# A two-layer decoder trunk on one core: the value projection cut in two, two more pairs of heads turned by DMA, copies moved off GpSimd, and a softmax written with a minimum

## The chip, the cores and the metric

The kernel runs on 1 core of a Trainium2 chip. The time is the device time of one execution in microseconds (us). The engines are TensorE (matmuls; PE in the profile, PEld for its weight loads), VectorE (DVE), ScalarE (ACT), GpSimd (POOL) and SyncE (SP), which here only issues DMAs. The kernel before took 558.63 us (median of 3 runs, 558.53 to 558.71).

## The reference

The model has 256 positions of width 1024 and two layers. Layer 0 mixes positions with a chunked gated MLP, layer 1 with attention of 16 heads of width 64. Each mixer is followed by a gated MLP with a causal convolution of width 3, and each of the four sub-layers ends in `x <- LayerNorm(alpha * x + f(x))`. Everything is float32.

What the change touches is the attention of layer 1. With 256 positions there is one key block, so each query sees its own block alone, under the causal mask and with a bias by distance:

```
qkv = (x @ w_qkv).reshape(B, S, 3, H, Dh)
s   = q * Dh**-0.5 @ k.T + bias[head, bucket(t - j)]      # -inf where j > t
p   = softmax(s)
o   = p @ v                                               # (S, H * Dh)
x   = layer_norm(alpha * x + o @ w_o, g, b)
```

## The kernel before

**Arithmetic.** A float32 product is built from three products of reduced-precision parts. Each operand is split into a high part and a low part (`split`, line 404): one copy on ScalarE or VectorE rounds to the high part, and one subtraction on VectorE gives the low part. A step of a projection is then high x high, high x low and low x high, all summed in one bank of PSUM. The weights are split in the same way as they arrive: `prep` (line 476) loads a 1 MB chunk into one of two raw buffers, ScalarE writes `whi` and VectorE writes `wlo`, 1024 columns at a time.

**The stream of weights.** All weight chunks stand in one list, `stream` (line 422), in the order of their use. The kernel holds five chunks (`CHUNKS`). When a chunk has been used, `spent` (line 514) starts the load and the split of the chunk five places further on. The attention stage uses four chunks of the value weights (`b_v`), then eight of query and key weights (`b_qk`, one chunk for one pair of heads), then four of the output projection (`b_o`).

**The planner.** The program does not write the order of the instructions directly. Every operation is recorded with an engine, a cost in ns, and what it reads and writes (`Plan.op`, line 96). `schedule` (line 178) then simulates the five engines with these costs and the order of each engine's instructions is what comes out. TensorE's operations are of two sorts. Bulk ones (the projections) keep the order in which they were recorded. Those marked `fill` (scores, products with the values, transposes) are put in between at the first moment when the simulation has their data ready. On the other engines the operation with the earliest due time goes first, and the due time is worked back from TensorE's operations. Once the order is fixed each engine runs its own instructions strictly in that order and waits on semaphores: where the chip is later than the simulation, the engine stands. A DMA is simulated as 1100 ns plus its bytes at 360 bytes per ns (line 236), and 910 ns later (line 91) its data count as there.

**The attention stage** (`moba`, line 998):

- The value projection comes first (lines 1018 to 1030): for each of 8 slices of the inner dimension and each half t of the positions, two outputs of 512 columns. Slices 0 to 4 are done for both halves, then 5 to 7. It holds four banks of PSUM (both tiles of two banks, `twos`). The second half of the positions is still being normalised and transposed when this projection begins; the first 30 matmuls are of the first half.
- `project(i)` (line 1033) computes queries and keys of pair i of heads, 16 matmuls of 512 columns and 16 of 256. `part` reads the two banks and splits the results.
- In the middle of the projection of pairs 2, 4 and 6 stand the scores of the two pairs before (`scores`, line 1059), and behind these the products with the values of the two pairs before those (`also`).
- `softmax` (line 1087) works in two pieces per head, 128 and 256 columns wide. VectorE adds the bias to the scores, reversed along the columns, and takes the maximum; a tiny VectorE instruction negates both maxima; ScalarE computes the exponential with that as its bias and sums it; VectorE takes the reciprocal and scales.
- The probabilities must be transposed before they meet the values. Pairs 0 to 3 (`BY_XBAR`) go through `turn_apart` (line 1113): a copy brings the low and the high 16-bit halves of the floats apart, a DMA transposes both planes of 16-bit elements, and a copy joins them. Of the two heads of a pair one goes by GpSimd and one by ScalarE, in both copies. Pairs 4 to 7 are transposed on TensorE (`turn`, line 1140), three 128 x 128 blocks for each head, and ScalarE copies the result out of PSUM.
- `apply` (line 1163) multiplies with the values; `keep` splits the result for the output projection.
- After the projection of pair 7 come the scores of pair 6 with the transposes of pairs 4 and 5, and the scores of pair 7 with the products of 4 and 5. The transposes and products of pairs 6 and 7 are placed behind given lengths of the output projection's matmuls (2600, 5800 and 9300 ns, lines 1193 and 1194).

**The output projection** (`project_out`, line 758, with `b_o`) has 8 slices, one for each pair of heads. It starts with slices 0 and 1, so the later pairs are needed only after a good part of its matmuls. Its four banks are given out in the order of `free` (line 765).

**Normalisation** (`stats`, line 614): after the statistics on VectorE one GpSimd instruction raises the variance to the power -1/2. The planner counts it as 465 ns (line 627).

Of the kernel before, what the change touches and what calls it, by code (L numbers as in the profile page):

```python
# [14 lines left out]
AF = mybir.ActivationFunctionType  # L15
# [4 lines left out]
P = 128  # L20
D = 1024
# [34 lines left out]
BY_XBAR = (0, 1, 2, 3)  # L56
# [207 lines left out]
def trunk_kernel(ctx: ExitStack, tc: tile.TileContext, a: dict, out: bass.AP):  # L264
# [163 lines left out]
    stream += [("b_v", c) for c in range(4)]  # L428
    stream += [("b_qk", c) for c in range(8)]
    stream += [("b_o", c) for c in range(4)]  # L430
# [183 lines left out]
    def stats(r, x, cuts, sum_into=None):  # L614
# [12 lines left out]
        plan.op("pool", 465, lambda: nc.gpsimd.tensor_tensor(rstd, ve, nhalf.ap, op=ALU.pow),  # L627
# [130 lines left out]
    def project_out(name, nk, at, xold, li, rows_i):  # L758
# [6 lines left out]
        free = [bank(True) for _ in range(2 * NT)]  # L765
        pieces = [[(o, HALF, free[2 * t + o // HALF]) for o in (0, HALF)] for t in range(NT)]
# [231 lines left out]
    def moba(h, l, scr):  # L998
        n4 = KT * S
        oh, ol = place("rr", 0, n4), place("rr", n4, n4)  # L1000
        pring = Places("ff", [17 * S + x * (P + S) for x in range(4)], P + S)
# [3 lines left out]
        ering = Places("ff", [4 * S + x * (P + S) for x in range(6)], P + S)  # L1005
# [10 lines left out]
        free_first = sorted(range(NT), key=lambda j: max(bank_of[i][0] for i in couple(j)))  # L1016
        pieces = [[(o, HALF, taken(i, True)) for o, i in zip((0, HALF), couple(j))] for j in free_first]
        for ks in (range(5), range(5, KT)):
            for t in range(NT):
                for k in ks:  # L1020
                    rows_step(pieces[t], *at(k, t), *sub("b_v", k // 2, k % 2), k == 0, k == KT - 1)
                    if t == NT - 1 and k % 2:
                        spent("b_v", k // 2)
                if ks[0] == 0 and t == 0:
                    plan.tick(AHEAD)
                if ks[0]:
                    for o, n, b in pieces[t]:
                        parts = [(t, i) for i in range(o // P, (o + n) // P)]
                        act(vv[:, t, o:o + n], b.ap, AF.Copy, [b], [(vb, parts)], psum=True)
                        done_with(b)  # L1030
# [28 lines left out]
        def scores(pairs, also=(), last=(), hold=None):  # L1059
# [15 lines left out]
            if hold is not None:  # L1075
                o.deps.add(hold)
            for i in pairs:
                held[i] = [softmax(bank2[i][hh], biases[i], hh) for hh in range(2)]
            if also:
                o = apply(also, o)  # L1080
# [6 lines left out]
        def softmax(b, bias, hh):  # L1087
# [209 lines left out]
```

## Time and profile before

| what | value |
|---|---|
| median of 3 runs | 558.63 us |
| the profiled execution | 558.67 us |
| its span, first to last instruction | 556.6 us |
| TensorE busy | 548.6 us, 3002 matmuls |
| VectorE busy | 474.8 us, 918 instructions |
| ScalarE busy | 378.9 us, 708 instructions |
| GpSimd busy | 24.1 us, 30 instructions |
| mean granted clock of TensorE | 0.997 of full speed |

Instructions on TensorE overlap, so its busy share says only that the engine had something in flight. Whether it sets the time is read from the chain that ended last: the profile follows the work back from the last instruction, at each step to what released it. A row of an engine's timeline gives start, length, engine, line, operation, the tiles written and read, their shapes, a count, and in brackets how long the engine stood before and what released it. Most matmuls carry line 365 and the transposes line 371, since helpers record them; so the tile names and shapes tell the stages apart. From 260.5 to 283.3 us runs the value projection, to 335.9 us the projections of queries and keys, then the output projection.

### The profile page before, as it was taken

The numbers are of one execution on the slowest core, as the hardware profiler recorded it, in microseconds if no ns is written. First come the engines' busy times: TensorE is split into PE (matmuls) and PEld (weight loads), VectorE is DVE, ScalarE is ACT, GpSimd is POOL, SyncE is SP. The second block draws the span as 40 slices with busy tenths as digits, with TensorE's granted clock in tenths as the row PEclk, the third lists the DMA queues.
The fourth block names the chain that finished last, engine by engine and source line by source line (L and its number), as shares of the span: only waits on it lengthen the run. The fifth ranks groups of instructions, "written<-read, shape, count | busy, mean of one in ns | idle before, by whom it ended". The sixth has DMA issues, their size and how long they took to land.

```text
span 556.6 us, 8330 instructions
## 1 busy us (share of the span) xinstructions
PE 548.6 (99%) x3002; PEld 469.2 (84%) x3002; DVE 474.8 (85%) x918; ACT 378.9 (68%) x708; POOL 24.1 (4%) x30
## 2 busy tenths in 40 slices
PE   9999999999999999999999999999999999999995
PEld 6889888888888888888888888788888988888884
DVE  5898989899989999668957978788999989999747
ACT  6657566977577877445567889576976677867621
POOL 0200210000000000001000310000000000000001
PEclk9999999999999999999999999999999999999998
DMA  8988428754655276862565783649655664466502
GB/s 324 412 304 315 172 75 218 286 215 152 221 200 185 80 262 231 281 252 77 226 227 184 189 198 112 228 155 284 240 190 162 220 222 155 151 232 237 212 0 76
DMA packets 30064, 113.58 MB, mean 204 GB/s; under 512 B 12790, under 2 KB 16072, under 8 KB 17864
## 3 DMA queue, kind: packets, MB, share of 16 engines
q1 hardware_dynamic: 29736, 112.80, 58.2%
q8 instruction: 23, 0.38, 0.3%
q10 hardware_dynamic: 288, 0.26, 0.1%
q14 instruction: 17, 0.14, 0.1%
HBM read 109.36 MB, written 1.07 MB: 198 GB/s over the span
## 4 chain that ended last, share of the span: by engine, by line
PE 88%; DVE 6%; DMA 3%; issue 1%; ACT 1%; POOL 0%; DVEq 0%; ACTq 0%; SPq 0%
PE bank L365 55%; PE twos L365 32%; DMA raw<-in_a_out 3%; DVE wlo L383 2%; PE bank L371 1%; DVE x L387 1%; DVE ff L387 1%; DVE stat L621 1%; DMA ff<-in_head 1%; ACT whi L377 0%; PE twos L371 0%; DVE rr L383 0%; POOL stat L627 0%; DVE stat L624 0%; DVE stat L661 0%
## 5 line engine op out<-in xcount | busy, mean ns | idle before, releaser
L383 DVE TENSOR_TENSOR wlo<-raw,whi 128x1024 fp32r<-128x1024 f32 (+1 forms) x202 | 219.3, 1114 | 16.9 <-ACT whi L377 16.6
L377 ACT ACTIVATE whi<-raw 128x1024 fp32r<-128x1024 f32 (+1 forms) x202 | 185.9, 966 | 40.6 <-DMA raw<-in_f_dn 13.6
L365 PE MATMUL bank<-whi,rr 128*128 128x512 f32 x432 | 136.0, 391 | 0.0
L365 PE MATMUL bank<-xt,whi 128*128 128x512 f32 x512 | 120.4, 390 | 0.0
L365 PEld LDWEIGHTS bank<-xt,whi 128*128 128x128 f32 x512 | 94.9, 188 | 19.1 <-issue 0.2
L365 PEld LDWEIGHTS bank<-whi,rr 128*128 128x128 f32 x432 | 81.1, 188 | 17.6 <-issue 0.5
L365 PE MATMUL bank<-wlo,rr 128*128 128x512 f32 x216 | 84.1, 389 | 0.0
L387 DVE SCALAR_TENSOR_TENSOR ff<-ff,convc 128x254 f32<-128x254 f32 (+1 forms) x176 | 76.2, 478 | 6.5 <-ACT ff L377 6.0
L365 PE MATMUL twos<-xt,whi 128*128 128x512 f32 x320 | 74.4, 390 | 0.0
L365 PEld LDWEIGHTS twos<-xt,whi 128*128 128x128 f32 x320 | 59.4, 188 | 11.9
L365 PEld LDWEIGHTS bank<-xt,wlo 128*128 128x128 f32 x512 | 64.0, 191 | 1.9 <-issue 0.2
L365 PE MATMUL bank<-xt,wlo 128*128 128x256 f32 x512 | 65.6, 284 | 0.0
L377 ACT ACTIVATE ff<-ff,convc 128x256 f32<-128x256 f32 x88 | 48.4, 591 | 1.8 <-DVE ff L383 1.7
L365 PEld LDWEIGHTS bank<-wlo,rr 128*128 128x128 f32 x216 | 40.6, 188 | 7.9
L377 ACT ACTIVATE ff<-bank 128x256 f32<-128x256 f32 (+2 forms) x62 | 24.0, 393 | 28.3 <-PE bank L365 25.5
L365 PE MATMUL twos<-whi,xt 128*128 128x512 f32 x128 | 41.5, 394 | 0.0
L365 PEld LDWEIGHTS twos<-xt,wlo 128*128 128x128 f32 x320 | 39.7, 192 | 0.8
L365 PE MATMUL twos<-xt,wlo 128*128 128x256 f32 x320 | 40.0, 283 | 0.0
L377 ACT ACTIVATE ff<-bank,lncol 128x128 f32<-128x128 f32 x48 | 18.8, 457 | 25.3 <-PE bank L371 20.8
L377 ACT ACTIVATE ff<-twos 128x512 f32<-128x512 f32 (+1 forms) x26 | 14.4, 568 | 25.5 <-PE twos L365 22.4
L365 PEld LDWEIGHTS twos<-whi,xt 128*128 128x128 f32 x128 | 24.1, 188 | 4.8
L627 POOL TENSOR_TENSOR stat<-stat,nhalf 128x1 f32<-128x1 f32 x9 | 9.1, 1011 | 420.1 <-DVE stat L626 420.1
(120 smaller groups left out, 543.2 us busy)
## 6 DMA issues: line engine op xcount, KB each, us to landing
raw<-in_f_up SPq DMA_DIRECT2D x44, 1024.0 KB, 4.8
raw<-in_f_dn SPq DMA_DIRECT2D x22, 1024.0 KB, 4.8
raw<-in_b_qk SPq DMA_DIRECT2D x8, 1024.0 KB, 4.8
lnrow<-in_lnrow SPq DMA_DIRECT2D x5, 1024.0 KB, 8.3
raw<-in_a_out SPq DMA_DIRECT2D x4, 1024.0 KB, 7.0
raw<-in_b_v SPq DMA_DIRECT2D x4, 1024.0 KB, 4.7
raw<-in_b_o SPq DMA_DIRECT2D x4, 1024.0 KB, 5.8
raw<-in_a_u SPq DMA_DIRECT2D x3, 1024.0 KB, 8.4
```

Source lines behind the costliest of these rows:

```text
L365: nc.tensor.matmul(o, l, x, start=start, stop=stop)
L371: nc.tensor.transpose(o, x, ident.ap)
L377: return plan.op("act", ns, lambda: nc.scalar.activation(o, x, func, **kw), r, w, table=table)
L383: return dve(70 + 1.04 * flat(x), lambda: nc.vector.tensor_tensor(o, x, y, op=op), r, w)
L387: lambda: nc.vector.scalar_tensor_tensor(o, x, s, y, op0=op0, op1=op1), r, w)
L621: dve(70 + 1.04 * n, lambda j=j, o=o, n=n: nc.vector.bn_stats(s[:, j, :], x[:, o:o + n]), [(r, range(o // S, (o + n) // S))], [(st, [("st" ...
L627: plan.op("pool", 465, lambda: nc.gpsimd.tensor_tensor(rstd, ve, nhalf.ap, op=ALU.pow), [(st, ["ve"]), nhalf], [(st, ["rstd"])])
```

## The change

- The value projection is cut into two halves of 512 output columns (heads 0 to 7, heads 8 to 15). The first stands where the whole stood, with the first half of the positions before the second; the other stands behind the projection of pair 7. The chunks of the value weights are laid out to match, and the last two stand behind the eight of queries and keys in the stream.
- Pairs 4 and 5 also go through `turn_apart`. Its copies are done by ScalarE for one head of a pair and by VectorE for the other; GpSimd does none. The joined probabilities go back to the buffers of the exponentials, of which there are ten and no longer six, and the separate ring for transposed probabilities is gone.
- The scores of pairs 6 and 7 are one visit. The products of pairs 0 and 1 stand behind the scores of 4 and 5, those of 2 and 3 behind the scores of 6 and 7. Behind the second half of the values come the products of 4 and 5, then the transposes and products of 6 and 7, each for two pairs at once and without given delays.
- The softmax keeps the negated sum of scores and bias, takes its minimum, and lets the exponential multiply by -1; the negation is gone, and each exponential depends on the minimum of its own piece alone.
- The planner counts GpSimd's power as 700 ns, and two of the output projection's banks are exchanged.

```diff
-BY_XBAR = (0, 1, 2, 3)
+ALSO = {4: (0, 1), 6: (2, 3)}
+TURNS = {}
+TURNS_BEHIND = {}
+LAST_TURN = (6,)
+APART_BY = ['act/dve', ...]
+JOINED_BY = ['dve/act', ...]
+BY_XBAR = (0, 1, 2, 3, 4, 5)
...
-    stream += [("b_v", c) for c in range(4)]
+    stream += [("b_v", c) for c in range(2)]
     stream += [("b_qk", c) for c in range(8)]
+    stream += [("b_v", c) for c in range(2, 4)]
...
-        plan.op("pool", 465, lambda: nc.gpsimd.tensor_tensor(rstd, ve, nhalf.ap, op=ALU.pow),
+        plan.op("pool", 700, lambda: nc.gpsimd.tensor_tensor(rstd, ve, nhalf.ap, op=ALU.pow),
...
         free = [bank(True) for _ in range(2 * NT)]
+        if name == "b_o":
+            free[1:3] = free[2:0:-1]
...
-        pring = Places("ff", [17 * S + x * (P + S) for x in range(4)], P + S)
...
-        ering = Places("ff", [4 * S + x * (P + S) for x in range(6)], P + S)
+        ering = Places("ff", [at + x * (P + S) for at, n in ((4 * S, 6), (17 * S, 4)) for x in range(n)], P + S)
...
+        def values(half_, bs, turns):
+            for t, ks in turns:
                 for k in ks:
+                    w = sub("b_v", 2 * half_ + k // 4, k // 2 % 2)
+                    rows_step([(k % 2 * HALF, HALF, bs[t])], *at(k, t), *w, k == 0, k == KT - 1)
+                    if t == NT - 1 and k % 4 == 3:
+                        spent("b_v", 2 * half_ + k // 4)
+                if half_ == 0 and t == 0:
                     plan.tick(AHEAD)
...
+        older = min(range(NT), key=lambda j: max(bank_of[i][0] for i in couple(j)))
+        values(0, [taken(i, True) for i in couple(older)], [(t, range(KT)) for t in range(NT)])
...
             for c, (cut, n) in enumerate(cuts):
                 dve(70 + 1.04 * n, lambda c=c, cut=cut: nc.vector.tensor_tensor_reduce(
-                    out=e.ap[:, cut], in0=b.ap[:, cut], in1=bv[:, hh, back[c]], scale=1.0, scalar=-3e38,
-                    op0=ALU.add, op1=ALU.max, accum_out=m[:, c:c + 1]), [b, bias], [(e, [c]), (sm, [c])])
-            dve(70, lambda: nc.vector.tensor_scalar_mul(m, m, -1.0), [(sm, [0, 1])], [(sm, [0, 1])])
+                    out=e.ap[:, cut], in0=b.ap[:, cut], in1=bv[:, hh, back[c]], scale=-1.0, scalar=3e38,
+                    op0=ALU.add, op1=ALU.min, accum_out=m[:, c:c + 1]), [b, bias], [(e, [c]), (sm, [c])])
             for c, (cut, n) in enumerate(cuts):
-                act(e.ap[:, cut], e.ap[:, cut], AF.Exp, [(e, [c]), (sm, [0, 1])], [(e, [c]), (sm, [2 + c])],
+                act(e.ap[:, cut], e.ap[:, cut], AF.Exp, [(e, [c]), (sm, [c])], [(e, [c]), (sm, [2 + c])], scale=-1.0,
                     bias=m[:, c:c + 1], accum=total[:, c:c + 1], table="exp")
...
-            ns = {"act": (860, 1080), "dve": (590, 620), "pool": (1500, 1500)}[e][not first]
+            ns = {"act": (860, 1080), "dve": (590, 620), "pool": (1050, 1050)}[e][not first]
...
-                by('pool/act', True, j, lambda f, j=j, e=e: f(ah[:, j], halves(e.ap)), [(e, [0, 1])], [(a, [j])])
+                by(APART_BY[i], True, j, lambda f, j=j, e=e: f(ah[:, j], halves(e.ap)), [(e, [0, 1])], [(a, [j])])
...
-                by('pool/act', False, j, lambda f, j=j, p=p: f(halves(p.ap), bh[:, j]), [b], [p])
-                held[i][j] = p
+            for j, p in enumerate(held[i]):
+                by(JOINED_BY[i], False, j, lambda f, j=j, p=p: f(halves(p.ap), bh[:, j]), [b], [(p, [0, 1])])
...
+        def visit(i):
+            return lambda hold: scores((i, i + 1), also=ALSO.get(i, ()), last=TURNS.get(i, ()), hold=hold)
+
         for i in range(PAIRS):
             if i in (2, 4, 6):
-                project(i, lambda hold: scores((i - 2, i - 1), also=(i - 4, i - 3) if i > 2 else (), hold=hold))
+                project(i, visit(i - 2))
                 continue
             end = project(i)
...
-        scores((n - 1,), last=(n - 3, n - 2), hold=end)
-        scores((n,), also=(n - 3, n - 2))
...
-        for ns, what, i in ((2600, turn, (n - 1,)), (5800, apply_and_turn, n - 1), (9300, apply, (n,))):
-            behind(ns, what, i)
+        visit(PAIRS - 2)(end)
+        values(1, [bank(True) for _ in range(NT)], [(t, range(KT)) for t in range(NT)])
+        for i in range(0, PAIRS, 2):
+            if all((i, i + 1) != x for x in ALSO.values()):
+                o = None
+                if i in LAST_TURN:
+                    o = turn((i, i + 1))
+                apply((i, i + 1), o)
...
-        "b_v": by_rows(qkv[:, 2 * D:]),
+        "b_v": f(qkv[:, 2 * D:].reshape(2, 2, 2, P, 2, HALF).transpose(4, 0, 3, 1, 2, 5).reshape(4, P, CH)),
```

More of the change, by code (lines that the diff above doesn't have):

```diff
@@ L1015, in moba @@
         at = xt_at(h, l)
[L1016 to L1019, printed above, removed]
+        def values(half_, bs, turns):
+            for t, ks in turns:
                 for k in ks:
[L1021 to L1024, printed above, removed]
-                    plan.tick(AHEAD)
[L1026 to L1030, printed above, removed]
+                    w = sub("b_v", 2 * half_ + k // 4, k // 2 % 2)
[3 more added lines that the diff above has]
+                if half_ == 0 and t == 0:
+                    plan.tick(AHEAD)
+                if ks[-1] == KT - 1:
+                    o = half_ * HALF
+                    parts = [(t, i) for i in range(o // P, (o + HALF) // P)]
+                    act(vv[:, t, o:o + HALF], bs[t].ap, AF.Copy, [bs[t]], [(vb, parts)], psum=True)
+                    done_with(bs[t])
+        older = min(range(NT), key=lambda j: max(bank_of[i][0] for i in couple(j)))
+        values(0, [taken(i, True) for i in couple(older)], [(t, range(KT)) for t in range(NT)])
         held, biases = {}, {}
@@ L1076, in scores @@
                 o.deps.add(hold)
+            if also:
+                o = apply(also, o)
             for i in pairs:
                 held[i] = [softmax(bank2[i][hh], biases[i], hh) for hh in range(2)]
-            if also:
-                o = apply(also, o)
             for i in pairs:
@@ L1135, in take @@
             for n, b in enumerate(bs):
-                p = pring.new()
-                act(p.ap, b.ap[:, :P + S], AF.Copy, [b], [p], psum=True)
-                held[pairs[n // 2]][n % 2] = p
+                p = held[pairs[n // 2]][n % 2]
+                act(p.ap, b.ap[:, :P + S], AF.Copy, [b], [(p, [0, 1])], psum=True)
         def turn(pairs, hold=None):
@@ L1148, in applied @@
         def applied(pairs):
-            b = half() if pairs[-1] == PAIRS - 3 else bank()
+            b = half() if pairs[-1] >= PAIRS // 2 else bank()
             w = [(b.ap[hh * DH:(hh + 1) * DH, n * S + at:(n + 1) * S],
@@ L1154, in applied @@
                  for c, (at, cut) in enumerate(((0, slice(0, S)), (P, slice(S, S + P)))) for hh in range(2)]
-            return b, w, [(vb, [(t, i) for t in range(NT) for i in pairs]), *(p for i in pairs for p in held[i])]
+            return b, w, [(vb, [(t, i) for t in range(NT) for i in pairs]), *((p, [0, 1]) for i in pairs for p in held[i])]
         def keep(pairs, b):
@@ L1169, in apply @@
             return o
+        def visit(i):
+            return lambda hold: scores((i, i + 1), also=ALSO.get(i, ()), last=TURNS.get(i, ()), hold=hold)
         for i in range(PAIRS):
             if i in (2, 4, 6):
-                project(i, lambda hold: scores((i - 2, i - 1), also=(i - 4, i - 3) if i > 2 else (), hold=hold))
+                project(i, visit(i - 2))
                 continue
             end = project(i)
-            if i in (3, 5) and i - 2 not in BY_XBAR:
-                turn((i - 3, i - 2), hold=end)
-        n = PAIRS - 1
-        scores((n - 1,), last=(n - 3, n - 2), hold=end)
-        scores((n,), also=(n - 3, n - 2))
-        def behind(ns, what, i):
-            def go():
-                last = next(o for o in reversed(plan.ops) if o.eng == "pe" and not o.fill)
-                what(i).after = last
-            plan.later(ns, go)
-        def apply_and_turn(i):
-            o = apply((i,))
-            turn((i + 1,), o)
-            return o
-        for ns, what, i in ((2600, turn, (n - 1,)), (5800, apply_and_turn, n - 1), (9300, apply, (n,))):
-            behind(ns, what, i)
+            if i in TURNS_BEHIND:
+                turn(TURNS_BEHIND[i], end)
+        visit(PAIRS - 2)(end)
[6 more added lines that the diff above has]
+                apply((i, i + 1), o)
         return lambda k, t: (ohv[:, k, t * P:(t + 1) * P], olv[:, k, t * P:(t + 1) * P],
```

8 lines of the change are left out of this document (3 added, 5 removed).

## The prediction

> **What bounds the kernel now.** I read the page first (busy shares, then the chain that ended last), then the chain in order of time around the attention stage, then the engines' timelines there.
>
> ```profile
> span 556.6 us, 8330 instructions
> PE 548.6 (99%) x3002; PEld 469.2 (84%) x3002; DVE 474.8 (85%) x918; ACT 378.9 (68%) x708; POOL 24.1 (4%) x30
> PE 88%; DVE 6%; DMA 3%; issue 1%; ACT 1%; POOL 0%; DVEq 0%; ACTq 0%; SPq 0%
> ```
>
> TensorE is 88% of the chain that ended last. The busy share alone would not prove that, so here is the chain itself, in order of time, from the end of the projections of queries and keys into the output projection (start us, length us, engine, tile, line, count):
>
> ```profile
> 325.26 1.35 PE twos L365 x19
> ...
> 335.95 0.78 PE twos L365 x9
> 336.73 0.89 PE bank L365 x3
> 337.62 0.66 PE bank L371 x6
> 338.27 0.66 PE twos L371 x6
> 338.93 0.69 PE bank L365 x3
> 339.62 0.78 PE twos L365 x9
> 340.39 0.91 PE bank L365 x3
> 341.30 1.45 PE twos L365 x16
> 342.75 2.96 PE bank L365 x12
> 345.71 0.66 PE twos L371 x6
> 346.37 2.08 PE bank L365 x9
> 348.44 0.80 PE twos L365 x8
> 349.24 0.91 PE bank L365 x3
> 350.15 0.66 PE twos L371 x6
> 350.81 1.40 PE bank L365 x6
> 352.20 0.80 PE twos L365 x8
> 353.00 9.09 PE bank L365 x39
> ...
> 490.26 51.72 PE bank L365 x228
> ```
>
> Every piece begins where the one before it ends, and none belongs to another engine: here TensorE is the path, and what leaves its queue leaves the time, provided that nothing then arrives late. "bank x..." are matmuls of the output projection, "twos x9" the scores of one pair of heads (x19 those of two pairs), L371 the transposes, "twos x8" and "x16" the products with the values for one pair and for two. The last row gives the steady price of a 512-column matmul: 51.72 / 228 = 0.227 us.
>
> **The change, part by part.**
>
> *TensorE's visits for pairs 4 to 7.* Before, eight visits: scores 6 (0.78), turn 4 and 5 (0.66 + 0.66), scores 7 (0.78), apply 4 and 5 (1.45), turn 6 (0.66), apply 6 (0.80), turn 7 (0.66), apply 7 (0.80): 7.25 us. After, four: scores 6 and 7 together (1.35, the first row), apply 4 and 5 (1.45), turn 6 and 7 together (1.32), apply 6 and 7 together (1.45): 5.57. That is 1.68 us less; the twelve transposes of pairs 4 and 5, which the DMA takes over, are 1.32 of it. The 78 matmuls between the visits take 0.89 + 0.69 + 0.91 + 2.96 + 2.08 + 0.91 + 1.40 + 9.09 = 18.93 us where 78 x 0.227 = 17.71 would do: 1.22 us over eight visits, 0.15 for each change of kind. Four fewer visits save 0.6. Bounds: -1.7 (no such saving) to -2.6 (the visits for pairs 0 to 3 also stand side by side more often). I take **-2.3**.
>
> *The value projection in halves.* It has 96 matmuls of 512 columns before and after, so the work is the same; 48 of them (48 x 0.227 = 10.9 us) move behind the last projection. There they cover the softmax of pairs 6 and 7, which the output projection covered before. In front, rows of the second half of the sequence are now needed after 24 matmuls and no longer after 30. The chip before was here:
>
> ```profile
> 266.92 0.48 PE L365 MATMUL twos<-whi,xt 128*128 128x512 f32 x1
> 267.23 0.42 DVE L383 TENSOR_TENSOR xt<-ff,xt 128x256 fp32r<-128x256 f32 x1
> ```
>
> The 25th matmul starts at 266.92, while the low part of the transposed input for the second half is written until 267.65. After the change the third matmul of the group that starts there wants it, at 266.92 + 2 x 0.227 = 267.37: 0.3 us of waiting if nothing else moves, 0 if VectorE gets to this chain sooner (the two chunks wanted first were split long before, and the splits that follow are not urgent). Bounds 0 to 0.7; I take +0.1.
>
> *The planner's 700 ns for GpSimd's power.* The place where the profile shows TensorE idle for this chain is the normalisation behind the first output projection:
>
> ```profile
> 69.54 0.93 POOL L627 TENSOR_TENSOR stat<-stat,nhalf 128x1 f32<-128x1 f32 x1 [9.05 <-DVE stat L626]
> 71.11 1.11 PE L371 MATMUL bank<-ident,x 128*128 128x128 f32 x8 [0.47 <-DVE x L390]
> ```
>
> Priced at 465 ns the transposes were put 0.47 us too early. 235 ns more in the plan puts them about a group of matmuls later, work that fills part of the gap. Bounds 0 and -0.5 (a shift in the order of VectorE's work could also lose as much, so +0.5 for the range); I take -0.2.
>
> *Copies and the negation.* VectorE gets 12 copies of 768 16-bit elements (GpSimd's eight and part of ScalarE's share, and those of pairs 4 and 5) and loses 16 negations; ScalarE goes from 8 such copies to 12 and loses 4 reads of 384 columns out of PSUM. The exponentials wait for their own piece's minimum only.
>
> ```profile
> 298.20:351.00 52.80, 52.80 (x372) 43.65 (x372) 45.64 (x170) 45.25 (x123) 7.50 (x8) 1.00 0.65 178
> L1103 DVE TENSOR_SCALAR ff<-ff,smax 128x256 f32<-128x256 f32 x16 | 6.4, 415 | 0.1
> L1097 DVE TENSOR_SCALAR smax<-smax 128x2 f32<-128x2 f32 x16 | 3.1, 239 | 0.0
> L1122 ACT COPY ff<-raw 128x768 uint16<-128x768 uint16 x2 | 2.1, 1070 | 0.0
> 348.73 2.35 DVE L383 TENSOR_TENSOR wlo<-raw,whi 128x1024 fp32r<-128x1024 f32 x2
> ```
>
> The first row is the stretch from the first scores to the last weight split of the output projection: its columns are length, then PE, PEld, DVE, ACT and POOL busy. VectorE works 45.6 of 52.8 us. After the change the stretch is 52.8 + 10.9 - 2.3 = 61.4 us; VectorE's load 45.6 - 3.1 + 4 x 1.2 (two value chunks are now split inside it, two pieces each; a piece is half of the fence's last row) + 12c = 47.3 + 12c, with c the price of a copy. No row has such a copy on VectorE: between 0.42 (its own scaling of 256 elements) and 1.07 (ScalarE's slower copy). I take 0.7, nearer to the first, which is the engine's own row. Idle left: 5.7 us, against 7.2 before. The cover is the lead of the weights: the last split ends at 351.1, and the matmul that first needs it is the 49th of the 78, the tenth of the last piece, 353.00 + 9 x 0.227 = 355.0: 4 us. So the copies cost nothing, and the negations gain nothing. The Trainium skill (VectorE: DVE Perf Modes, What auto-detection actually checks) says that a one-input copy inside SBUF uses both read ports where the outermost dimensions are even, whatever its step. An estimate from that page's clock and fixed part is 768 / 2 / 0.96 ns + 156 ns = 0.56 us, and by it 7.4 us would be left idle; no run here shows it yet.
>
> *The moved DMAs.* SP issues six transposing DMAs where it issued four, and two value chunks behind the eight of queries and keys. Behind a waiting transpose on SP's queue stand the biases and the loads of the output projection, which had a lead of 4 us even as splits. What is not covered is where the plan lets TensorE arrive:
>
> ```profile
> 316.00 1.06 ACT L1122 COPY ff<-raw 128x768 uint16<-128x768 uint16 x1
> 317.99 1.52 PE L365 MATMUL bank<-ff,lnrow 128*64 128x256 f32 x16
> 321.91 1.29 SPq L420 DMA_TRANSPOSE apart<-apart  x1
> 327.08 1.08 ACT L1122 COPY ff<-apart 128x768 uint16<-128x768 uint16 x1 [1.42 <-DMA apart<-apart]
> ...
> apart<-apart SPq DMA_TRANSPOSE x2, 3.9
> raw<-in_b_qk SPq DMA_DIRECT2D x8, 1024.0 KB, 4.8
> ```
>
> The products for pairs 0 and 1 began 0.93 us after their last copy. The plan holds a copy to be possible 1.1 + 1.1 + 0.9 = 3.1 us after the issue (lines 236 and 91); the chip needed 5.2 (1.29 to issue, 3.9 to land), and ScalarE stood 1.42 us. GpSimd's copies were planned at 1.5 us, which hid this; at 0.62 for VectorE the plan comes 0.88 us earlier, and the margin of 0.93 is spent. Pairs 0 to 3 get a whole visit more of time, so only pairs 4 and 5 are exposed, and behind them the turn and the products of 6 and 7, which lose their written delays. Each of these, and the joint scores, can wait 0 to 0.5 us; together 0 to 2.0, and I take +0.5. The Trainium skill (Advanced Engine Details and Errata, X-Bar Transpose (TRN2)) says that transposing DMAs are as fast as regular ones. The trace agrees in part only: 0.39 MB (128 x 1536 x 2 bytes) turned land after 3.9 us, where 1 MB loaded lands after 4.8. By the rule the plan's 3.1 would about hold, this allowance would fall away, and the time would be 556.3.
>
> **Sum.** -2.3 + 0.1 - 0.2 + 0.5 = -1.9. The profiled execution took 558.67 (span 556.6 and 2.07 around it), 0.04 above the median. 558.67 - 1.9 = **556.8 us**.
>
> **Rivals.**
>
> *TensorE arrives too early* (the plan's clock). For it: the spent margin and the 1.42 us. Against: with so many products moved back, few visits remain exposed. At its price of 1.5 to 2.0 in place of 0.5 the time is 558.0: no change.
>
> *VectorE becomes the bound* (the slower side). Its queue is in order, and a copy that waits for a DMA now holds up weight splits and the reading of the query and key banks behind it. Place: the output projection's weights. If the 7.2 us of gaps must stay, VectorE is late by 7.2 - (14.1 - 12c), which passes the lead of 4 us from c = 0.91. At c = 1.07 it is 1.9 us over, and two waits of 1.42 for DMAs make it 4.8: 556.3 + 4.8 = 561.1 (the 0.5 above is then inside it). Against it: c would have to be as slow as ScalarE's.
>
> *The removed work was hidden anyway.* The chain leaves no room for it: no other engine appears between 335.95 and 362.09. I give it nothing of its own.
>
> **How the numbers follow.** The forecast, 0.60, has its own range of 555.8 to 557.5; early arrival, 0.25, 557.3 to 559.0; VectorE as the bound, 0.15, 559 to 562. The range takes the first two whole, the low ends of the costs (-2.6 and -0.5 without waits: 555.5) and a small part of the third: 555.4 to 559.7. A measurement of this kernel tells about 0.2%, 1.1 us, from no change: faster means below 557.5. That is the forecast and a sixth of early arrival, 0.63; within it 0.24; slower 0.13.
>
> **What would show it.** Right: in the chain of the new profile one piece of scores "x19" behind the eighth projection, then value matmuls, one apply, one L371 pair and one apply, no L371 for pairs 4 and 5, and no engine but TensorE from 71 us to the last layer's end; the attention stage about 2 us shorter; the gap before the first transposes at 71 us smaller. Wrong: TensorE idle with a releaser in ScalarE's or VectorE's joins (the plan was early); TensorE waiting for the output projection's low weights (VectorE is the bound); VectorE copies above 0.9 us; or a different first 70 us, where the path is not TensorE's and the plan's new price may reorder work.

## The result and the profile after

The changed kernel takes 555.42 us (median of 6 runs, 555.21 to 556.12) against 558.67 us (median of 6 runs, 558.53 to 559.95) for the kernel before on the same chip: a ratio of 0.9939, 95% interval 0.9926 to 0.9952, which is 2.7 to 4.1 us faster. The forecast was 556.8 in a range of 555.4 to 559.7: the direction was right and the gain was larger. The ratio applied to the 558.63 us on which the forecast rests gives 555.2, a little below the range. Three executions in the runs below took more than twice the usual time; they are left out of the times, and where one of them was the profiled one, no profile is used.

First the page of the changed kernel: its span, the busy time of each engine, and the engines' shares of the chain that ended last.

```profile
span 553.6 us, 8263 instructions
PE 546.0 (99%) x2990; PEld 467.9 (85%) x2990; DVE 477.8 (86%) x914; ACT 381.4 (69%) x708; POOL 16.5 (3%) x22
PE 92%; DVE 5%; DMA 2%; issue 0%; ACT 0%; POOL 0%; DVEq 0%; ACTq 0%
```

TensorE has twelve matmuls fewer, which are the transposes of pairs 4 and 5, and a larger share of the chain. Nothing in these three rows says where the time went. For that the reader compares two chains between the same two landmarks: the transposes of the normalisation ahead of the attention stage and the first gates' products of the MLP behind it. Before:

```profile
255.50 0.87 PE bank L371 x8
...
379.15 11.09 PE bank L365 x64
```

After, with the attention stage between them (start us, length us, engine, tile, line, count; 371 is now the matmuls' line and 377 that of the transposes):

```profile
255.17 0.87 PE bank L377 x8
...
313.90 11.86 PE bank L371 x76
325.76 1.35 PE twos L371 x20
327.11 11.20 PE bank L371 x58
338.31 1.45 PE twos L371 x16
339.76 1.59 PE bank L371 x6
341.35 1.31 PE twos L377 x12
342.66 2.75 PE bank L371 x12
345.41 1.45 PE twos L371 x16
346.86 12.47 PE bank L371 x54
359.32 0.87 PE bank L377 x8
...
376.35 11.09 PE bank L371 x64
```

From landmark to landmark the stage took 379.15 - 255.50 = 123.65 us before and 376.35 - 255.17 = 121.18 after: **2.47 us less**. This length is called "the stage" below. All other stretches between such landmarks agree within 0.1 us. The profiled execution became 3.30 us shorter (558.67 to 555.37). Beside the stage, 0.33 of that is the time to the first bank of TensorE's matmuls (5.03 and 4.70 us), 0.30 lies outside the span, and 0.20 is left over. The start is not put down to the change: over the kernels below, which share it, it lay between 5.00 and 5.36 us. The part outside the span is steady: 1.68 to 1.77 us in all six runs of the changed kernel, 2.00 to 2.13 in every run of the kernel before that was timed beside the kernels below. It differs by kernel without an order that these runs explain (2.04 on average with the products of 0 to 3 offered earlier, the only edit). So of a measured gain of 2.7 to 4.1 us the trace shows 2.5 in the stage; 0.3 goes with the kernel for a reason that stays open, and the rest is not attributed.

After the eighth projection the chain has the four visits forecast: scores of 6 and 7 (1.35), products of 4 and 5 (1.45), transposes (1.31) and products (1.45) of 6 and 7; the 58 matmuls between the first two hold the products of 2 and 3, the rest of the value projection and six of the output projection. TensorE stands for nobody in the stage. Its list of waits over the whole span (releaser, total us, times, longest) is

```profile
PE twos L1212 <- PEq L1288: 0.8, 1, 0.8
PE bank L371 <- DVE whi L414: 0.4, 1, 0.4
PE bank L377 <- DVE x L396: 0.3, 1, 0.3
```

and the last is the gap at 71 us. Next, what the forecast doubted, the margin of pairs 4 and 5. The engines' timelines of the changed kernel:

```profile
70.84 1.11 PE L377 MATMUL bank<-ident,x 128*128 128x128 f32 x8 [0.28 <-DVE x L396]
332.76 1.08 ACT L1130 COPY ff<-raw 128x768 uint16<-128x768 uint16 x1
332.92 0.61 DVE L1130 COPY ff<-raw 128x768 uint16<-128x768 uint16 x1
336.99 0.60 ACT L383 ACTIVATE lnrow<-bank 128x512 f32<-128x512 f32 x1 [0.59 <-PE bank L371]
338.24 1.52 PE L371 MATMUL twos<-ff,lnrow 128*64 128x256 f32 x16
```

The last join of pair 5 ends at 332.76 + 1.08 = 333.84, and the products of 4 and 5 start at 338.24: 4.4 us later. What they follow closely is another producer, ScalarE's copy of the second half of the values out of PSUM, which ends at 336.99 + 0.60 = 337.59. Last, the price of a copy on VectorE (groups: busy us, mean ns), of a scaling, and the stretch from the scores of pairs 0 and 1 to the last weight split (length, then PE, PEld, DVE, ACT, POOL):

```profile
L1127 DVE COPY apart<-ff 128x768 uint16<-128x768 uint16 x3 | 1.7, 552 | 0.0
L1130 DVE COPY ff<-raw 128x768 uint16<-128x768 uint16 x3 | 1.8, 615 | 0.4 <-DMA raw<-raw 0.4
L1112 DVE TENSOR_SCALAR ff<-ff,smax 128x256 f32<-128x256 f32 x16 | 5.1, 342 | 0.0
287.10:348.00 60.90, 60.90 (x410) 50.77 (x410) 53.82 (x173) 53.63 (x131) 0.00 (x0) 1.00 0.71 203
```

A copy takes 0.55 to 0.62 us where 0.7 was assumed, and VectorE keeps 60.9 - 53.8 = 7.1 us idle where 5.7 was forecast.

### The profile page after: what moved, and what is told of

The parts are those of the page before. It is cut to its first block, busy times and chain, and to the rows that moved or that the text cites. A ratio compares the mean times of both kernels' runs of the same rounds, so it can differ in the third digit from the quotient of the medians.

```text
span 553.6 us, 8263 instructions
## 1 busy us (share of the span) xinstructions
PE 546.0 (99%) x2990; PEld 467.9 (85%) x2990; DVE 477.8 (86%) x914; ACT 381.4 (69%) x708; POOL 16.5 (3%) x22
## 3 DMA queue, kind: packets, MB, share of 16 engines
HBM read 109.36 MB, written 1.07 MB: 199 GB/s over the span
## 4 chain that ended last, share of the span: by engine, by line
PE 92%; DVE 5%; DMA 2%; issue 0%; ACT 0%; POOL 0%; DVEq 0%; ACTq 0%
PE bank L371 60%; PE twos L371 30%; DVE wlo L389 2%; DMA raw<-in_a_out 1%; PE bank L377 1%; DVE x L393 1%; DMA ff<-in_head 1%; DVE stat L628 0%; DVE ff L389 0%; DVE ff L393 0%; DVE rr L389 0%; PE twos L377 0%; ACT whi L383 0%; POOL stat L634 0%; DVE stat L668 0%
## 5 line engine op out<-in xcount | busy, mean ns | idle before, releaser
L393 DVE SCALAR_TENSOR_TENSOR ff<-ff,convc 128x255 f32<-128x255 f32 (+1 forms) x176 | 76.6, 477 | 7.1 <-ACT ff L383 6.7
L383 ACT ACTIVATE ff<-bank 128x256 f32<-128x256 f32 (+1 forms) x60 | 23.2, 391 | 29.7 <-PE bank L371 23.3
L371 PE MATMUL twos<-whi,xt 128*128 128x512 f32 x96 | 31.4, 395 | 0.0
L371 PE MATMUL bank<-whi,xt 128*128 128x512 f32 x96 | 29.1, 393 | 0.4 <-DVE whi L414 0.4
L383 ACT ACTIVATE ff<-ff 128x256 f32<-128x256 f32 x52 | 19.9, 410 | 10.4 <-DVE rr L389 8.6
```

The costliest lines, as they stand in the source:

```text
L371: nc.tensor.matmul(o, l, x, start=start, stop=stop)
L383: return plan.op("act", ns, lambda: nc.scalar.activation(o, x, func, **kw), r, w, table=table)
L393: lambda: nc.vector.scalar_tensor_tensor(o, x, s, y, op0=op0, op1=op1), r, w)
```

## The experiments

The theory under test: the gain is the visits that leave TensorE, and every other part is about free. The rivals: single parts have prices of their own, hidden in the whole; or they need one another. Ratios are to the kernel before, timed beside each run.

### The start of the plan: GpSimd's price

Edit to the changed kernel: `plan.op("pool", 700, ...)` back to 465.

> The changed kernel with one number taken back: the planner counts GpSimd's power as 465 ns again. Theory (the price of 700 is worth what the first 71 us show): the first matmul behind the transposes of the first normalisation starts at 71.98 us as in the kernel before, not at 71.70, and the time is 555.4 + 0.3 = 555.7 us; the attention stage keeps its length within 0.1 us. Rival (the 0.3 us come from elsewhere, a shifted order or the chip): it stays at 71.7 and 555.4.

555.73 us, ratio 0.9944 (0.9930 to 0.9958). The stage is 121.18 us, and the transposes behind the first output projection start at 71.31 us against 70.84; with the 700 ns kept, the other kernels below that build on the changed one have this start between 70.7 and 71.5. The new price is worth nothing that shows.

### Parts taken out of the changed kernel

**Pairs 4 and 5 back on TensorE.**

```diff
-LAST_TURN = (6,)
-BY_XBAR = (0, 1, 2, 3, 4, 5)
+LAST_TURN = (4, 6)
+BY_XBAR = (0, 1, 2, 3)
```

> The changed kernel with pairs 4 and 5 transposed on TensorE again, as one visit of twelve blocks. Theory (what TensorE no longer does is the gain, and nothing waits): one visit comes back, 1.31 us in the chain and 0.15 for the change of kind, so +1.5 us, 556.9. Rival (the DMA way has hidden costs, in waits or in VectorE's copies, that go away here): less than +1.0, below 556.4.

> The changed kernel with pairs 4 and 5 turned on TensorE as before, for a profile of it. Theory (the half of the values behind the projections gives the cover, and the DMA way of 4 and 5 is worth its twelve transposes and a visit): no wait of TensorE over 0.3 us, the stage 122.5 to 122.9 us against 121.18. Rival (the half behind is worth its cover to the DMA way alone, and on TensorE the transposes stand between other work for nothing): the stage below 122.2.

557.21 us, ratio 0.9972 (0.9960 to 0.9984), and the same kernel once more 557.43 us, ratio 0.9976 (0.9965 to 0.9986). In the profile of the second the chain has one more visit, and TensorE stands for nobody in the stage:

```profile
333.33 1.31 PE twos L377 x12
...
343.83 1.31 PE twos L377 x12
```

The stage is 122.53 us, 1.35 longer than 121.18; the visit's own 1.31 is nearly all of it, and only 0.04 is left for the changes of kind. That is the visits' account of the prediction, alone.

**All eight pairs by DMA.** `LAST_TURN = ()`, `BY_XBAR = (0, ..., 7)`.

> The changed kernel with pairs 6 and 7 turned by DMA too, so that no transposes of probabilities are left on TensorE. Theory: another visit goes, 1.31 + 0.15 us, and the products of 6 and 7, which the way over copies, DMA and joins brings some 20 us behind their scores (326), come at about 347, before the output projection needs them at 352 (its 49th matmul): 555.4 - 1.5 = 553.9. Rival (this way is too long behind the last scores): TensorE waits for the joins of 6 and 7 or for the split of their products, 1 to 4 us, so 555 to 558.

560.49 us, ratio 1.0029 (1.0018 to 1.0040). Twelve further transposes leave TensorE and the kernel becomes slower than before. There is no profile of it to use, so which wait it was isn't shown.

**The copies back on GpSimd** (`'act/dve'` and `'dve/act'` to `'pool/act'`; the planner's 1050 ns kept).

> The changed kernel with the twelve copies of VectorE on GpSimd, planned at 1.05 us each. Theory (the copies lie beside TensorE's work wherever they run): 555.4, within 0.7, and the small VectorE instructions that run beside a GpSimd copy take longer, as before (0.86 us for a negation, 1.0 for a scaling). Rival (taking GpSimd out was part of the gain): over 556.5.

557.72 us, ratio 0.9983 (0.9974 to 0.9992); the stage is 122.38, 1.20 longer. The waits of TensorE and the scaling in this kernel:

```profile
PE bank L371 <- DVE wlo L389: 0.7, 1, 0.7
L1112 DVE TENSOR_SCALAR ff<-ff,smax 128x256 f32<-128x256 f32 x16 | 5.7, 367 | 0.1
L1112 DVE TENSOR_SCALAR ff<-ff,smax 128x128 f32<-128x128 f32 x16 | 5.5, 355 | 0.0
```

TensorE waits for VectorE's low weights of the second half of the values. VectorE's scaling of 256 columns takes 367 ns on average in the kernel with GpSimd's copies, 342 in the one without; the 128-column one 355 against 276. One row shows it alone: the scaling of 128 columns that starts at 295.41, inside a GpSimd copy that runs from 295.29 to 296.17, lasts 0.85 us. The Trainium skill (SBUF — State Buffer, Who interferes with whom) says that GpSimd and VectorE share one pair of ports, and that where an instruction of VectorE uses it too, the one that starts first holds it for its whole instruction; the two means and the row agree with the direction. How much of the 1.20 us comes from this and how much from the other order of the plan is not separated.

**The negation back** (maximum, a negation in an instruction of its own, each exponential behind both pieces).

> As the changed kernel, but the softmax takes the maximum and negates it in an instruction of its own, sixteen of some 0.24 us on VectorE, and each exponential waits for both pieces. Theory (the removed negations were hidden): the attention stage 121.1 to 121.4 us, time 555.2 to 556.0. Rival (VectorE's idle time is on the way to pair 7's weights and joins): a wait of TensorE for VectorE, the stage 121.8 or longer, time 556.2 to 557.5.

556.42 us, ratio 0.9963 (0.9950 to 0.9977); the stage is 121.68, 0.50 longer. One wait has appeared:

```profile
342.16 1.20 PE twos L377 x9
...
PE twos L377 <- DVE rr L389: 0.3, 1, 0.3
```

Nine of the twelve transposes of 6 and 7 need banks that VectorE is still splitting the products of 4 and 5 out of. So the negation wasn't quite hidden. The order of the plan differs here too (the joint scores stand about 2 us later in the stage), so how much of the 0.5 is the sixteen instructions and how much the other order is not settled.

**Pairs 6 and 7 apart** (scores, transposes and products in visits of one pair).

> The changed kernel with pairs 6 and 7 apart: scores, transposes and products for one pair at a time, three visits more. By the prediction's price: scores 0.78 + 0.78 in place of 1.35, transposes 0.66 + 0.66 in place of 1.32, products 0.80 + 0.80 in place of 1.45, so 0.36 us of work and 3 x 0.15 for changes of kind: +0.8 us, 556.2. Rival (joining visits is worth nothing): 555.4. If the pairs apart wait for each other's banks, more than 556.8.

556.74 us, ratio 0.9970 (0.9958 to 0.9981). The stage is 122.39, 1.21 longer, without a wait of TensorE in it. The work is the same but for shapes (two scores of 0.78 for one of 1.35, two products of 0.80 for one of 1.45, transposes 0.65 + 0.66 for 1.31: 0.36 more), so three more visits cost 0.85, or 0.28 each; the prediction had 0.15 for a change of kind.

**Two more variations of the order.** Products of 0 to 3 offered one visit earlier (`ALSO = {2: (0, 1), 4: (2, 3)}`), and the products of 4 and 5 recorded right behind the transposes of 6 and 7.

> As the changed kernel, but the products of pairs 0 and 1 are offered one visit earlier, behind the scores of 2 and 3, and those of 2 and 3 behind the scores of 4 and 5, as in the kernel before. Theory of the prediction (the plan holds a DMA transpose to be done 2 us before the chip has it, and without GpSimd's slow copies nothing hides this): TensorE stands 0.5 to 1.0 us before the products of 0 and 1 and again before those of 2 and 3, the stage 122.0 to 123.2 us, time 556.2 to 557.4. Rival (the plan places them late enough): no wait over 0.2 us, one or two changes of kind more, the stage 121.2 to 121.6, time 555.3 to 555.9.

> As the changed kernel, but the products of pairs 4 and 5 stand right behind the transposes of 6 and 7, one visit fewer. Theory (a change of kind costs TensorE about 0.15 us, and nothing waits): the attention stage 120.9 to 121.1 us against 121.18, time 555.1 to 555.5. Rival (the joined visit comes before the softmax of pair 7 is through, or the products of 6 and 7 come later): a wait of TensorE of 0.3 us or more at the joined visit, time 555.8 to 556.5.

The first: 557.05 us, ratio 0.9969 (0.9957 to 0.9981), the stage 121.68. TensorE waits for nobody, so the prediction's early arrival does not show even here: the last joins end at 304.70 and 319.63, and the products start at 305.72 and 320.75, 1.0 and 1.1 us later. The products now stand in the middle of projections, away from other visits, as in the kernel before; in the changed kernel they follow scores directly (313.90 and 327.11). So two separate visits cost 0.50 here. The timed runs are 1.6 above the changed kernel's: beside the 0.5 of the stage, 0.3 is the part outside the span and 0.35 the start of TensorE's work; the remaining 0.5 isn't explained (the profiled execution, 556.59, is the fastest of its five). The second: 555.43 us, ratio 0.9943 (0.9931 to 0.9956), the stage 120.77. The chain joins the products of 4 and 5 to those of 6 and 7, one piece of 2.75 us for two of 1.45. One visit fewer saved 0.41 in the trace, 0.15 of it in that piece; the time can't be told from the changed kernel's.

### Both halves of the values in front

```diff
-    stream += [("b_v", c) for c in range(2)]
+    stream += [("b_v", c) for c in range(4)]
     stream += [("b_qk", c) for c in range(8)]
-    stream += [("b_v", c) for c in range(2, 4)]
...
         values(0, [taken(i, True) for i in couple(older)], [(t, range(KT)) for t in range(NT)])
+        values(1, [taken(i, True) for i in couple(1 - older)], [(t, range(KT)) for t in range(NT)])
...
-        values(1, [bank(True) for _ in range(NT)], [(t, range(KT)) for t in range(NT)])
```

> The changed kernel with both halves of the value projection in front of queries and keys, and the weights in that order. In the changed kernel the products of pairs 4 and 5 start 4.4 us after their last joining copy, since the second half of the values is copied out of PSUM only 0.65 us before them. Theory (that copy, not the written plan, protects these products): here nothing but the joins holds them, their margin falls from 4.4 us to under 1 us, a wait of TensorE up to 0.5 us may show there, and the time is 555.4 to 556.4. Rival (moving the half is itself worth something as cover for the last softmax): TensorE waits more than 1 us behind the last scores, time over 556.5.

561.04 us, ratio 1.0040 (1.0027 to 1.0054): slower than the kernel before, with every other part of the change in it. The stage is 126.51, **5.33 longer**. In its timeline:

```profile
328.04 1.07 ACT L1130 COPY ff<-apart 128x768 uint16<-128x768 uint16 x1 [1.58 <-DMA apart<-apart]
328.04 0.61 DVE L1130 COPY ff<-apart 128x768 uint16<-128x768 uint16 x1 [1.92 <-DMA apart<-apart]
...
337.12 0.49 PE L371 MATMUL twos<-ff 64*128 64x128 f32 x4 [1.24 <-DVE ff L393]
```

ScalarE and VectorE both stand for a transposing DMA, the reading of pair 7's queries and keys is behind them in their queues, and TensorE, done with the eighth projection, stands 1.24 us before pair 7's part of the joint scores. The forecast margin did fall: the last join of pairs 4 and 5 ends at 342.16 and their products start at 342.47. But TensorE does not stand for them; the waits are elsewhere, and the time is the rival's. TensorE's waits in the stage add up to 2.9 us. One of 0.7 is for a bank in front, where the two halves stand together, and it comes back below in the kernel before with its values cut; so not all of the 5.33 is want of cover at the end. Three kernels asked what in the front placement does the rest.

With pairs 4 and 5 on TensorE as well:

> The value projection whole in front, as in the run before this (561.0 us), and pairs 4 and 5 transposed on TensorE again. Theory now: the half behind the projections covers the waits that the DMA way of pairs 4 and 5 puts into VectorE's and ScalarE's queues; without that way the waits (some 4.5 us in that run) go and one visit of 1.5 us comes: 556.5 to 558.5. Rival (the waits come from the products and the joint scores standing together at the end, whatever the turning): it stays at 560 to 562.5.

562.56 us, ratio 1.0075 (1.0055 to 1.0095), the stage 126.14. The profiled execution (560.66) was the fastest; the two others took 562.56 and 562.95. TensorE still waits, 2.0 us behind the eighth projection, which the list puts down to ScalarE's parts of pair 7, so the DMA way of 4 and 5 is not what makes them late. With GpSimd's copies instead:

> The value projection whole in front, pairs 4 and 5 by DMA, and the copies apart and together on GpSimd for one head of a pair and ScalarE for the other, as the kernel before had them. If the load of VectorE (12 copies of 0.55 to 0.6 us, 7 us) makes the waits, they shrink: 556 to 558.5. If the cause is that VectorE and ScalarE stand for a DMA that lands later than planned, half of it is left: ScalarE still stands, VectorE not: 558 to 560. If neither, 561.

563.34 us, ratio 1.0089 (1.0074 to 1.0104), the stage 128.63: 3.0 us of waiting for VectorE's parts, worse than any branch expected. With the ending of the kernel before:

> Both halves of the values in front, and the ending as in the kernel before: scores of pair 6 and of pair 7 apart, transposes and products of 6 and 7 apart behind written delays in the output projection; pairs 4 and 5 still by DMA, copies on ScalarE and VectorE. Theory (the half behind is worth its cover only because the scores of 6 and 7 are joint; the old ending had its cover from the output projection): no wait of TensorE over 0.3 us between 326 and 350 us, the attention stage 121.7 to 122.4 us (123.65 before, less 1.32 for the twelve transposes and two visits at 0.15), time 556.0 to 557.2. Rival (with the copies and joins on ScalarE and VectorE the values in front leave these two too late whatever the ending): waits of 1 us or more behind the eighth projection, the stage 123.5 or longer, time 558.5 to 561.

560.13 us, ratio 1.0030 (1.0020 to 1.0039), the stage 125.35. My theory, that the joint scores alone needed the cover, fell. So none of the three explanations held, and what exactly the half behind covers is not isolated. Its waits of TensorE:

```profile
PE twos L371 <- ACT lnrow L383: 0.7, 1, 0.7
PE twos L371 <- DVE qk L389: 0.6, 1, 0.6
PE twos L371 <- ACT qk L383: 0.5, 1, 0.5
```

### Single parts added to the kernel before

The two values halves, both in front (the new `values`, called twice):

> The kernel before with one part alone: the value projection in two halves of the columns, both in front. Theory (the second half needs banks that ScalarE has still to empty, as in the runs with both halves in front, and nothing else changes): one wait of TensorE for ScalarE's value copies of 0.7 to 0.9 us at about 278 us, the attention stage 124.2 to 124.7 us against 123.65, time 559.2 to 559.9. The prediction's step (0.1, bounds 0 to 0.7): the stage 123.6 to 124.0, time 558.6 to 559.1.

559.90 us, ratio 1.0021 (1.0011 to 1.0030), the stage 124.81. The chain names the wait forecast: TensorE needs a bank that ScalarE has still to empty. So cutting the values and leaving both halves in front costs 1.16 us of the stage by itself.

```profile
278.99 0.61 ACT lnrow L377
```

Pairs 4 and 5 by DMA, copies on GpSimd and ScalarE:

> The kernel before with one part alone: pairs 4 and 5 turned by DMA, with copies on GpSimd and ScalarE as for pairs 0 to 3. Theory (twelve transposes leave TensorE and nothing arrives late): the stage 122.0 to 122.4 us against 123.65, time 556.9 to 557.5. Rival (without a half of the values behind the projections, the joins of 4 and 5 hold ScalarE when the banks of pair 7 have to be read, or the products of 4 and 5 come too early): waits of TensorE of 1 us or more after 334 us, the stage 123.2 to 125, time 558.2 to 560.

560.56 us, ratio 1.0032 (1.0020 to 1.0045), the stage 125.51: 1.86 longer although twelve transposes are gone. TensorE waits in the output projection:

```profile
PE bank L365 <- DVE rr L383: 1.4, 1, 1.4
PE bank L365 <- ACT rr L377: 0.5, 1, 0.5
```

The copies of pairs 0 to 3 on ScalarE and VectorE:

> The kernel before with one part alone: the copies before and behind the DMA transposes of pairs 0 to 3 on ScalarE and VectorE, none on GpSimd. Theory of the prediction (TensorE is the path and the copies fit into VectorE's idle time): the stage 123.5 to 123.9 us, time 558.3 to 559.0. Rival (a copy that waits for a DMA on VectorE holds up what stands behind it, or the products come before the joins): waits of TensorE of 0.5 us or more, the stage 124.2 to 125.5, time 559.2 to 560.5.

562.10 us, ratio 1.0059 (1.0044 to 1.0074), the stage 127.27, worse than both branches. VectorE's timeline shows a copy that stands for its DMA, and the chain that ended last runs over such a DMA, VectorE and ScalarE until matmuls of the output projection at 341.27:

```profile
330.36 0.63 DVE L1122 COPY ff<-apart 128x768 uint16<-128x768 uint16 x1 [1.74 <-DMA apart<-apart]
```

```profile
324.71 5.62 DMA apart<-apart
...
330.36 0.04 DVE ff L1122
...
334.78 3.00 ACT ff L377 x13
...
341.27 0.97 PE bank L365 x3
```

This is the mechanism of the prediction's slower rival (a copy that waits for a DMA holds up an engine's queue), at another place: the parts of pair 7, not the output projection's weights. But TensorE's waits behind it are only 0.9 us. The longest comes earlier:

```profile
PE bank L365 <- DVE rr L383: 2.1, 1, 2.1
```

It ends at 325.87, in the middle of a projection, and the list puts it down to VectorE's split of products. ScalarE's part of that split (from 324.37) stands behind its two copies apart (322.91 to 324.47), VectorE's (from 325.05) behind its own two (324.10 to 325.11). So the larger part of TensorE's 3.0 us stands behind copies made before a DMA, not behind one that waits for it.

And the half of the values behind the projections, with nearly all else as before (4 and 5 on TensorE, copies on GpSimd and ScalarE, negation, eight visits):

> The second half of the values behind the projections, and little else of the change: pairs 4 and 5 turned on TensorE, copies on GpSimd and ScalarE at the old planned cost, maximum and negation, scores, transposes and products of 6 and 7 apart (eight visits). Theory (the half behind saves nothing by itself; it is cover, which the other parts use): the stage 123.3 to 124.1 us against 123.65, time 558.2 to 559.2. Rival (the kernel before already lost time for want of cover, and the half alone gains): the stage below 122.9, time below 558. Second rival (the parts add: what each cost when it was taken out of the changed kernel, 1.35 + 1.20 + 1.21 + 0.50, comes on top of 121.18): the stage 125 or longer, time above 560.

558.54 us, ratio 0.9994 (0.9984 to 1.0003); the stage is 123.62 against 123.65. By itself it is worth nothing.

### The parts together

| part | added alone to the kernel before: stage, ratio | taken out of the changed kernel: stage, ratio |
|---|---|---|
| (kernel itself) | 123.65 | 121.18, 0.9939 |
| second half of the values behind | 123.62, 0.9994 | 126.51, 1.0040 |
| pairs 4 and 5 by DMA | 125.51, 1.0032 | 122.53, 0.9976 |
| copies off GpSimd | 127.27, 1.0059 | 122.38, 0.9983 |
| minimum for negation | not run alone | 121.68, 0.9963 |
| 6 and 7 in joint visits | not run alone | 122.39, 0.9970 |

The DMA way and the copies cost 1.9 and 3.6 us alone and gain 1.35 and 1.2 in the whole. Whether the place of the half turns the sign of the DMA way is not settled. With the half behind, the DMA way changes the stage from 122.53 to 121.18. With the values in front, the traces have 126.14 without it and 126.51 with it, a loss of 0.4, but the timed runs say the opposite, 562.56 us without and 561.04 with it (the trace of 126.14 is of an execution 1.9 us faster than the two others). For the copies the place of the half does not turn the sign: with the values in front they still gain (128.63 with GpSimd's, 126.51 without). So which part of the change turns either sign stays open. The row of 126.51 also holds the price of two halves together in front, 1.16 by the single part, since no run has the rest of the change with the values uncut. What stands is that the half gains nothing alone, and that all the other parts, with the cut values in front, are slower than the kernel before; less 1.16 the stage would be 125.35, still longer than 123.65 (an estimate from the two traces). The exchange of two banks and the ten buffers were not run alone.

## Where the prediction was wrong, and where it was right

**The visits, -2.3: right.** Eight visits of 7.25 us became four of 5.56 (forecast 5.57), and TensorE stands nowhere in the stage on either side, so the stage's 2.47 is this term: 1.69 of work and 0.78 for fewer visits. These are six and not four, since the products of pairs 0 to 3 no longer stand alone inside a projection either; the prediction had that as its bound of -2.6, and those two cost 0.50 when they were put back. Over six visits 0.78 is 0.13 each, where 0.15 was read; six visits at 0.15 would have given -2.6, so it is partly luck that -2.3 comes this close. The stage is inside the bounds of this term.

**Moved DMAs and early arrival, +0.5: the step that failed.** It measured 0. "Only pairs 4 and 5 are exposed" overlooked that their products also read the second half of the values, which leaves PSUM only at 337.59. That holds them 4.4 us behind their joins, and the margin of 0.93 - 0.88 never comes to bear. Nor is the margin spent where nothing else holds the products: with those of 0 to 3 offered earlier it is 1.0 and 1.1 us, and with the values in front 0.3 us for pairs 4 and 5, without a wait of TensorE for a join. So "the plan comes 0.88 us earlier, and the margin of 0.93 is spent" did not come about; why the margin of 0 to 3 stayed is not shown. The DMAs themselves stayed about as slow as the step had them, by their rows in the list of the changed kernel's DMAs (median us from issue to landing):

```profile
apart<-apart SPq DMA_TRANSPOSE x3, 3.8
raw<-raw SPq DMA_TRANSPOSE x3, 4.4
```

The time that the rule of equal speed would have given (556.3) came nearer, but not by its reason.

**Halves +0.1 and the planner's price -0.2: both 0.** The half adds no wait in the whole, and the price none that shows. These two cancel nearly; without the +0.5 the sum would have been -2.4, as the stage has it.

**Around the span, 2.07: taken over unchanged.** The prediction kept the time outside the span without a reason. It is 1.68 to 1.77 us in every run of the changed kernel, 0.3 less. Of the distance from the stage's 2.47 to the 3.25 between the medians, some 0.8 us, this is the part that goes with the kernel; its cause and the other 0.5 stay open.

**Copies and negation, "the copies cost nothing, and the negations gain nothing": right as a cost, wrong as a worth.** At 0.55 to 0.62 us a copy, VectorE keeps its idle time. The Trainium skill's estimate (VectorE: DVE Perf Modes, What auto-detection actually checks) was 0.56, and the trace agrees: 0.552 and up to 0.615. But GpSimd's copies left in place would have cost 1.2 us, and the negation 0.5 (with the order of the plan that comes with each). The prediction asked what the new copies cost, and not what the old ones would cost in the new order.

**The values, "the work is the same": true, and the larger miss of the reasoning.** It was priced as a place where something may arrive late. In fact the rest of the change gains only with the half behind: 5.33 us lie between the two placements, of which 1.16 is what two halves together in front cost by themselves, and the ten microseconds of matmuls behind give nothing by themselves. The prediction did name it as cover for the softmax of 6 and 7, and gave that no number.

**The rivals.** Early arrival did not occur. VectorE as the bound did not occur in the whole; with the copies alone TensorE waited 3.0 us for VectorE, though not for weights. The signs named as right all came (one visit of scores for 6 and 7 behind the eighth projection, no transposes of 4 and 5, no other engine in the stage's chain), except the smaller gap at 71 us: 0.28 after 0.47 in these two profiles, but 0.37 with the old price and 0.5 in a kernel with the new one (pairs 6 and 7 apart), so it is no sign of the price.

## What to carry to other kernels

Where TensorE is the path and has no idle time before or after, count all its visits and their work, also those that only move next to others: the count here came within 0.2 us and still missed two. Then try each part both alone and taken out, since a part can cost 1.9 us alone and gain 1.35 in the whole. Before a margin between two producers is called spent, list every operand of the consumer: the latest one may be another. And judge a small difference by the timed runs beside the trace: one trace here was of an execution 1.9 us faster than the two others of its kernel.

## What the runs showed of the hardware

A copy of 768 16-bit elements per partition with a step takes VectorE 0.552 us (apart) and 0.607 to 0.615 (join) on average, where ScalarE takes 0.82 to 0.83 and 1.07. In the kernel whose copies run on GpSimd, VectorE's scaling of 128 columns takes 355 ns on average and not 276, and one that started inside such a copy took 0.85 us. A separate visit of TensorE cost between 0.04 and 0.28 us beyond its own work, by its place. A transposing DMA of 0.39 MB landed 3.8 to 4.4 us (median) after its issue.
